# First two u tiles side by side from small loads, spreading products inside later tiles, second B table loaded early

## The chip, the cores and the metric

The kernel runs on one core of a Trainium2 chip. The metric is the time of one execution on the device in microseconds (us), as the median of several runs. The engines are TensorE (PE, with its weight loads PEld), VectorE (DVE), ScalarE (ACT), GpSimd (POOL) and SyncE (SP), which only issues transfers. A profile is one profiled execution; its times count from the start of its span.

## The reference

A decoder block in float32 on 528 tokens (16 meta tokens and 512 of the sequence) of width 1024:

```
xn = rmsnorm(h);  proj = xn @ w_in          # q, k, v, r, a_low, u, z_gla, z_ssm
o  = gla_chunked(q, k, v, log_sigmoid(a_low @ w_gate_up + b_gate) / 16)
y_gla = (rmsnorm(o) * silu(r)) @ w_o_gla
y_s = s5_ssm(u, ...)                         # 64 groups of 16 channels, 64 complex states each
y_ssm = GLU of gelu(y_s) @ w_glu + b_glu
h = h + rmsnorm((sigmoid(z_gla) * y_gla + sigmoid(z_ssm) * y_ssm) @ w_out)
h = h + rmsnorm(square(relu(rmsnorm(h) @ w_ff1)) @ w_ff2)
```

In `s5_ssm` the input matrix of each group is `Bbar = f * B` with complex f and B: `bb_re = fr * br - fi * bi`, `bb_im = fr * bi + fi * br`.

## The kernel before, in words

Every large product is made three times over. A float32 operand is split into a high half (`split_hi`, a ScalarE copy to the reduced type) and a low half (VectorE, operand minus high half), and `mm3` adds hi*hi, hi*lo and lo*hi in PSUM. A weight tile is 1024 x 128: eight k of 128 rows. `raw_w` loads it (tag `wraw`, three buffers, 512 KB) on SyncE's queue, `split_w` makes `whi` and `wlo` (three buffers each). Tokens come in two halves, 0 to 255 and 256 to 527 (`HALVES`), so a tile of one half is 24 matmuls of 256 or 272 columns.

In the first stage VectorE and ScalarE instructions are held in the program's order (`InOrder`), as are PE's (`pinned`); outside of it a scheduler orders the instructions of each engine by its own model of times, and may put later work ahead. `tc.issue_after(ins)` puts what is traced in its block behind `ins` on the same engine.

**Start (lines 452 to 660).** `u` is the first projection wanted. Its first five tiles of 128 columns are computed before the row norms are known: from x times the norm's gain (`rh`, `rl`, made by `taken_raw(k, q)` for one k and one half), and each result is multiplied by the row scale when it is taken from PSUM (`u_took`). The transposed tokens `x_cols0` come in four loads of two k each and the first weight tile in two of four k each, in turn on SyncE's queue; the second weight tile follows whole, then the second half of the tokens, a table for the S5 parameters, the third weight tile, and the token rows (three buffers `xt`). `busy` issues products of a constant tile so that PE has work until then. For each pair of k: two `taken_raw`, then `split_part` of the first weights; after these the first tile's 24 matmuls, then the second weight tile is split, then its 24 matmuls, then both tiles for the second half of the tokens.

`squared(i)` makes the sum of squares of token tile i on ScalarE, in place, and so frees a row buffer in the end; `rooted` makes the reciprocal roots (ScalarE's Sqrt and five small VectorE operations); `spread(q)` is a short PE product that spreads the row scales of half q over all partitions; `rows_of(q)` copies them from PSUM. Then `scaled`, `high` and `low` make the normalized x in halves (`xh`, `xl`), which everything later reads. `spread(0)` stands ahead of the third u tile, `spread(1)` ahead of the fourth. `work(us)` takes small VectorE operations for the S5 parameters from the list `jobs` until their estimated costs are used up.

**Early tiles (lines 663 to 895).** Ten calls of `early_slot(before, after)` follow, numbered 0 to 9 here; call n makes the matmuls of dense tile n (three u tiles, then seven gates of 24 matmuls of 512 columns). Between the high and the low half of the weights for tile n + 2 it does `before` of the jobs, and after the low half `after` of them. The jobs are here the powers of lambda, `b_bar`, the sums of the decay logarithms and so on. Seven of the calls stand in the block whose pools `qc` and `q5` close at lines 894 and 895, three behind it (lines 1251 to 1253).

**Second B table (lines 1242 to 1249).** `BA` holds the first B table, loaded early. Behind the seventh call the pool `b5` of the S5 blocks is open; the loads of the first block's `B` and `lam` are issued on GpSimd, and `other`, the second B table (`b_cols[1]`, 512 KB), is loaded on SyncE's queue into the buffer with the tag M3, which the blocks use later. Three jobs make `BA = BA * fr + other * fi`; four more make the first block's tables M2 and M1 (`tables`), of which M1 reads `B` and `lam`. Then the eight S5 blocks run beside the four heads; block 0 needs BA in `kernels`, its `E` (filled by `turns`, L1106) and `U` (eight loads, L1110) and M1 in `scan`.

Of the kernel before, what the change touches and what calls it, by code (L numbers as in the profile page):

```python
# [50 lines left out]
def hybrid_block(ctx: ExitStack, tc: tile.TileContext, io, out: bass.AP):  # L51
# [29 lines left out]
    def mk(pool, shape, dt=F32, tag=None, **kw):  # L81
        count[0] += 1
        name = f"{tag or 'x'}_{count[0]}"
        size = 1
        for n in shape[1:]:
            size *= n
        if pool not in lined or size % LINE == 0:
            return pool.tile(shape, dt, tag=tag or name, name=name, **kw)
        t = pool.tile([shape[0], -(-size // LINE) * LINE], dt, tag=tag or name, name=name, **kw)[:, :size]
        if len(shape) == 2:  # L90
            return t
        dims = " ".join("abcd"[: len(shape) - 1])
        return t.rearrange(f"p ({dims}) -> p {dims}", **dict(zip("abcd", shape[1:])))
# [23 lines left out]
    V.memset(warm, 1.0)  # L117
    S.activation(warm, warm, AF.Sqrt)
    epst = mk(cst, [P, 1], tag="epst")
# [10 lines left out]
    def bank(tag="sm"):  # L130
        return mk(ps_mm if tag == "mm" else ps_sm, [P, 512], tag=tag)
# [327 lines left out]
    rh, rl = (mk(pxt, [P, KT, LINE + SEQ], F32R, tag=t)[:, :, :NT] for t in ("rh", "rl"))  # L459
    raws, xts, loaded = [mk(wp, [P, KT, P], tag="wraw", bufs=3)], {}, None  # L460

    def behind():
        return tc.issue_after(loaded.ins) if loaded else ExitStack()

    for k in range(0, KT, 2):
        with behind():
            loaded = nc.sync.dma_start(xT[:, k : k + 2, :256], io["x_cols0"][:, k : k + 2])  # L467
        if k % 4 == 0:
            with behind():
                loaded = nc.sync.dma_start(raws[0][:, k : k + 4], w_in[k * P : (k + 4) * P, C_U : C_U + P].rearrange("(k p) n -> p k n", p=P))  # L470
    idle = bank()
# [12 lines left out]
    early = []  # L484
    for kind, i in (("u", 1), ("h", 0), ("h", 4), ("a", 0), ("u", 2), ("x", 0), ("x", 1), ("x", 2), ("x", 3), ("x", 4), ("u", 3), ("u", 4), ("w", 0), ("g", 0), ("u", 5), ("c", 0), ("u", 6), ("u", 7)):
        with behind():
# [84 lines left out]

    def raw_product(w, q, ps):
        a, b = HALVES[q]
        feat_tile(w, rh, rl, a, b, ps[:, : b - a])

# [6 lines left out]
    w0, w1 = (tuple(mk(wp, [P, KT, P], F32R, tag=t, bufs=3) for t in ("whi", "wlo")) for _ in range(2))  # L582
    for k in range(0, KT, 2):
        for i in range(2):
            taken_raw(k + i, 0)
        split_part(w0, raws[0], slice(k, k + 2))
    pair = bank("mm")
    raw_product(w0, 0, pair)
    for k in (0, 4):
        split_part(w1, raws[1], slice(k, k + 4))  # L590
    raw_product(w1, 0, pair[:, 256:])
    for k in range(KT):
        taken_raw(k, 1)
    last = {0: bank("mm"), 1: bank("mm")}
    raw_product(w0, 1, last[0])
    raw_product(w1, 1, last[1])
    w2_ = split_w(raws[2])
    squared(0)
    squared(1)
    rooted(slice(0, 2))  # L600
    V.tensor_copy(tri, trif)
    work(1.6)
    squared(2)
    ps = spread(0)
    rows_of(0, ps)
    pair2 = bank("mm")
    raw_product(w2_, 0, pair2)
    for i in range(2):
        u_took(pair[:, 256 * i : 256 * i + 256], uts[i], 0, True)
    squared(3)  # L610
    squared(4)
    scaled(0, range(0, 4))
    rooted(slice(2, TT + 1))
    w3 = split_w(raws[3])
    scaled(0, range(4, 8))
    high(0, range(0, 4))
    last[2] = bank("mm")
    raw_product(w2_, 1, last[2])
    ps = spread(1)
    low(0, (0, 2))  # L620
    raw_product(w3, 0, pair2[:, 256:])
    w4_hi = split_w_hi(raws[4])
    high(0, range(4, 8))
    rows_of(1, ps)
    w4 = w4_hi, split_w_lo(raws[4], w4_hi)
# [175 lines left out]
    with tc.issue_after(loaded.ins):  # L801
        nc.sync.dma_start(bn, io["b_rows"])
    nc.gpsimd.dma_start(kpad.rearrange("(t g) h l -> (g h) t l", g=GB)[:, :, :112], zpad)
    bar = mk(q5, [P, T8, 2, N], tag="bar")
    fb = mk(q5, [P, 2, N], tag="fb")
    lam = mk(q5, [P, 2, 9, N], tag="lamp")

    def powers_begun():
# [81 lines left out]
    work(2.4)  # L890
    early_slot(2.5, 2.2)
    early_slot(2.2, 100.0)
    assert not jobs
# [349 lines left out]
    first = blocks[0].tables()  # L1243
    other = mk(b5, [P, GB, P], tag="M3", bufs=1).rearrange("p a b -> p (a b)").rearrange("p (g h) -> p g h", h=HG)
    nc.sync.dma_start(other.rearrange("p g h -> p (g h)"), io["b_cols"][1])
    fr, fi = (prm[:, i, :].unsqueeze(2).to_broadcast([P, GRP, HG]) for i in range(2))
    jobs.append((1.2, lambda: V.tensor_mul(BA, BA, fr)))
    jobs.append((1.2, lambda: V.tensor_mul(other, other, fi)))
    jobs.append((1.2, lambda: V.tensor_add(BA, BA, other)))
    jobs.extend((c, lambda: next(first, None)) for c in (2.6, 1.4, 1.2, 2.6))  # L1250
    early_slot(2.2, 2.2)
    early_slot(2.2, 2.2)
# [422 lines left out]
```

## Time and profile before

| | us |
|---|---|
| median of 3 runs | 880.61 (880.41 to 881.18) |
| the profiled execution | 881.0 |
| its span | 879.3 |
| PE busy | 864.8 |
| VectorE busy | 653.0 |
| ScalarE busy | 442.7 |

A row of the timeline is: start, duration, engine, line, operation, output<-inputs, sizes, how many were merged, and in brackets the idle time of the engine before it and what ended it. SPq, ACTq, DVEq and POOLq are the queues in which an engine issues transfers or waits. Most instructions of the first stage have line 79 or 61, those of the helpers that record them, so they are told apart by the names of their tiles: `rh`, `rl` are x times the gain in halves, `whi`, `wlo` the weights in halves, `xrs` the row scales, `M` stands for M1, M2 and M3 (and for `other`, which lies in M3's buffer), `BA` is the B table. A row of the windows has the busy time of each engine in a stretch, the clock that PE was granted as a share of full speed, the busy share of the transfer engines and GB/s.

### The profile page before, as it was taken

The page shows a single profiled execution, that of the slowest core. Times are in us where ns is not written, and L with a number is a line of the kernel's source. Part 1 is how long each engine was busy: PE and PEld are TensorE (multiplying, and loading weights), DVE is VectorE, ACT ScalarE, POOL GpSimd, SP SyncE. Part 2 cuts the span into 40 slices and gives each one's busy share as a digit, 9 for nine tenths or more (in the row PEclk, how much of TensorE's full clock was granted, in tenths as well). Part 3 has the DMA queues.
Part 4 walks back from the last instruction along what each step waited for, and adds up shares of the span by engine and source line. Part 5 has one row for each costly group of instructions (what it writes and reads, how often), then busy time and mean ns, then how long its engine had stood idle before and what let it go on. Part 6 is the DMA issues. An engine that isn't in the chain of part 4 may idle for free.

```text
span 879.3 us, 13267 instructions
## 1 busy us (share of the span) xinstructions
PE 864.8 (98%) x4824; PEld 739.0 (84%) x4824; DVE 653.0 (74%) x1180; ACT 442.7 (50%) x749; POOL 121.8 (14%) x214
## 2 busy tenths in 40 slices
PE   8999899999999999999999999999999999999996
PEld 7998798999988888888888888988888888888885
DVE  6999789969695789956445765576666677688886
ACT  7677356767564545435333544333222236665763
POOL 1123120121213221342000001021112100000001
PEclk9999899999999999999999999999999999999998
DMA  8866785654555766758545761598999967856564
GB/s 289 262 198 190 219 191 135 165 141 133 143 133 149 221 170 190 197 159 278 178 143 169 216 191 52 182 319 291 336 302 305 319 238 223 279 194 195 172 206 144
DMA packets 166841, 180.57 MB, mean 205 GB/s; under 512 B 17992, under 2 KB 126696, under 8 KB 166776
## 3 DMA queue, kind: packets, MB, share of 16 engines
q1 hardware_dynamic: 147720, 117.26, 45.8%
q0 software_dynamic: 17744, 58.52, 19.9%
q10 hardware_dynamic: 1312, 3.94, 1.4%
q8 instruction: 38, 0.62, 0.3%
q14 instruction: 27, 0.22, 0.1%
HBM read 143.74 MB, written 35.95 MB: 204 GB/s over the span
## 4 chain that ended last, share of the span: by engine, by line
PE 92%; DMA 3%; DVE 2%; ACT 2%; SPq 1%; issue 1%; DVEq 0%; POOL 0%
PE mm L61 68%; PE sm L61 23%; PE sm L66 2%; DMA B<-bard 1%; DMA U<-ud 1%; DMA wraw<-in_w_in_dram 1%; ACT ga L79 0%; SPq L1110 0%; DVE b L79 0%; ACT whi L79 0%; ACT L79 0%; DVE c L1596 0%; SPq L467 0%; DVE wlo L79 0%; ACT prm L79 0%
## 5 line engine op out<-in xcount | busy, mean ns | idle before, releaser
L161 ACT ACTIVATE whi<-wraw 128x1024 fp32r<-128x1024 f32 x87 | 92.2, 1059 | 217.0 <-PE mm L61 191.8
L176 DVE TENSOR_TENSOR wlo<-wraw,whi 128x1024 fp32r<-128x1024 f32 x87 | 106.3, 1222 | 103.5 <-ACT whi L161 103.2
L61 PE MATMUL mm<-xh,wlo 128*128 128x512 f32 (+2 forms) x464 | 157.2, 339 | 3.2 <-DVE wlo L79 3.2
L61 PE MATMUL mm<-xh,whi 128*128 128x512 f32 (+2 forms) x464 | 159.9, 345 | 0.0
L61 PE MATMUL mm<-xl,whi 128*128 128x512 f32 (+2 forms) x464 | 156.6, 337 | 0.0
L61 PE MATMUL mm<-hh,whi 128*128 128x512 f32 (+1 forms) x280 | 104.0, 371 | 0.0
L61 PE MATMUL mm<-hl,whi 128*128 128x512 f32 (+1 forms) x280 | 103.8, 371 | 0.0
L61 PE MATMUL mm<-hh,wlo 128*128 128x512 f32 (+1 forms) x280 | 103.8, 371 | 0.0
L61 PEld LDWEIGHTS mm<-xh,wlo 128*128 128x128 f32 x464 | 88.2, 190 | 13.0 <-DVE wlo L79 3.7
L61 PEld LDWEIGHTS mm<-xh,whi 128*128 128x128 f32 x464 | 88.3, 190 | 9.7 <-issue 1.2
L61 PEld LDWEIGHTS mm<-xl,whi 128*128 128x128 f32 x464 | 88.2, 190 | 8.7
L1533 DVE TENSOR_TENSOR wlo<-wraw,whi 128x1024 fp32r<-128x1024 f32 x56 | 68.4, 1222 | 22.4 <-ACT whi L1529 22.1
L61 PE MATMUL sm<-whi,fl 128*128 128x512 f32 x192 | 74.8, 390 | 0.0
L61 PE MATMUL sm<-wlo,fh 128*128 128x512 f32 x192 | 74.8, 390 | 0.0
L61 PE MATMUL sm<-whi,fh 128*128 128x512 f32 x192 | 74.7, 389 | 0.0
L1529 ACT ACTIVATE whi<-wraw 128x1024 fp32r<-128x1024 f32 x56 | 58.7, 1049 | 19.2 <-PE mm L61 11.7
L61 PEld LDWEIGHTS mm<-hh,whi 128*128 128x128 f32 x280 | 52.7, 188 | 9.1
L61 PEld LDWEIGHTS mm<-hh,wlo 128*128 128x128 f32 x280 | 52.7, 188 | 9.0
L61 PEld LDWEIGHTS mm<-hl,whi 128*128 128x128 f32 x280 | 52.7, 188 | 9.0
L161 ACT ACTIVATE fh<-f 128x512 fp32r<-128x512 f32 x48 | 30.3, 631 | 43.4 <-PE sm L61 28.1
L61 PE MATMUL mm<-gh,whi 128*128 128x512 f32 x128 | 49.8, 389 | 0.0
L61 PE MATMUL mm<-gl,whi 128*128 128x512 f32 x128 | 49.8, 389 | 0.0
(408 smaller groups left out, 1773.1 us busy)
## 6 DMA issues: line engine op xcount, KB each, us to landing
wraw<-in_w_ff_dram SPq DMA_DIRECT2D x56, 512.0 KB, 5.7
wraw<-in_w_in_dram SPq DMA_DIRECT2D x47, 512.0 KB, 4.0
w2raw<-in_w_ff_dram POOLq DMA_DIRECT2D x16, 1024.0 KB, 8.9
t2d<-w2t POOLq DMA_DIRECT2D x16, 1024.0 KB, 5.9
wraw<-t2d SPq DMA_DIRECT2D x32, 512.0 KB, 3.7
wraw<-in_w_glu_dram SPq DMA_DIRECT2D x16, 512.0 KB, 4.2
M<-kpad POOLq DMA_DIRECT2D x64, 64.0 KB, 2.7
wraw<-in_w_o_gla_dram SPq DMA_DIRECT2D x8, 512.0 KB, 6.2
```

Source lines behind the costliest of these rows:

```text
L61: ins = nc.tensor.matmul(*args, **kw)
L66: ins = nc.tensor.transpose(*args, **kw)
L161: S.activation(dst, src, AF.Copy, scale=scale)
L176: V.tensor_sub(lo, raw, f32(hi))
L1529: halved = S.activation(bh, raw, AF.Copy)
L1533: V.tensor_sub(bl, raw, f32(bh))
```

## The change

Four things change.

- The first two u tiles are computed side by side: for each k the three matmuls of the first and the three of the second, into two PSUM banks (`side_by_side`), in both halves of the tokens. The first two k of both weight tiles are loaded on ScalarE's queue, the rest on SyncE's between the tokens; the first two k of the tokens come one by one. The weights are split in parts 0 to 1, 2 to 3 and 4 to 7, each after one `taken_raw`. The warming Sqrt of ScalarE, which loads its table, goes behind its two loads.
- `spread(0)` and `spread(1)` go into the third and fourth u tiles, ahead of their k = 3. `rooted` for the later tokens goes behind the fourth weight tile's split and two more scalings. Two results go to the other PSUM tag.
- `other` gets a place of its own in the pool `q5` and is loaded behind `bn` ahead of the early tiles. The three jobs go ahead of what was the seventh call of `early_slot`.
- One call of `early_slot` more stands ahead of the closing of the pools, and one fewer behind it.

```diff
--- before.py
+++ after.py
@@ -115,7 +115,6 @@
 
     warm = mk(cst, [P, 1], tag="warm")
     V.memset(warm, 1.0)
-    S.activation(warm, warm, AF.Sqrt)
     epst = mk(cst, [P, 1], tag="epst")
     V.memset(epst, EPS)
     ident = mk(cst, [P, P], tag="ident")
@@ -457,17 +456,24 @@
     nc.scalar.dma_start(g8, io["g_cols"])
     xT = mk(pxt, [P, KT, NT], tag="xT")
     rh, rl = (mk(pxt, [P, KT, LINE + SEQ], F32R, tag=t)[:, :, :NT] for t in ("rh", "rl"))
-    raws, xts, loaded = [mk(wp, [P, KT, P], tag="wraw", bufs=3)], {}, None
+    raws, xts, loaded = [mk(wp, [P, KT, P], tag="wraw", bufs=3) for _ in range(2)], {}, None
 
     def behind():
         return tc.issue_after(loaded.ins) if loaded else ExitStack()
 
-    for k in range(0, KT, 2):
+    def first_w(queue, i, k, n):
+        return queue.dma_start(raws[i][:, k : k + n], w_in[k * P : (k + n) * P, C_U + i * P : C_U + (i + 1) * P].rearrange("(k p) n -> p k n", p=P))
+
+    first_w(nc.scalar, 0, 0, 2)
+    held = first_w(nc.scalar, 1, 0, 2)
+    with tc.issue_after(held.ins):
+        S.activation(warm, warm, AF.Sqrt)
+    for i, k, n in (("x", 0, 1), ("x", 1, 1), (0, 2, 2), ("x", 2, 2), (1, 2, 2), ("x", 4, 2), (0, 4, 4), (1, 4, 4), ("x", 6, 2)):
         with behind():
-            loaded = nc.sync.dma_start(xT[:, k : k + 2, :256], io["x_cols0"][:, k : k + 2])
-        if k % 4 == 0:
-            with behind():
-                loaded = nc.sync.dma_start(raws[0][:, k : k + 4], w_in[k * P : (k + 4) * P, C_U : C_U + P].rearrange("(k p) n -> p k n", p=P))
+            if i == "x":
+                loaded = nc.sync.dma_start(xT[:, k : k + n, :256], io["x_cols0"][:, k : k + n])
+            else:
+                loaded = first_w(nc.sync, i, k, n)
     idle = bank()
 
     def busy(n, cols=256):
@@ -482,7 +488,7 @@
         return nc.sync.dma_start(xt[:n], io["meta_tokens"] if t == TT else io["x"][0, t * P : (t + 1) * P, :])
 
     early = []
-    for kind, i in (("u", 1), ("h", 0), ("h", 4), ("a", 0), ("u", 2), ("x", 0), ("x", 1), ("x", 2), ("x", 3), ("x", 4), ("u", 3), ("u", 4), ("w", 0), ("g", 0), ("u", 5), ("c", 0), ("u", 6), ("u", 7)):
+    for kind, i in (("h", 0), ("h", 4), ("a", 0), ("u", 2), ("x", 0), ("x", 1), ("x", 2), ("x", 3), ("x", 4), ("u", 3), ("u", 4), ("w", 0), ("g", 0), ("u", 5), ("c", 0), ("u", 6), ("u", 7)):
         with behind():
             if kind == "x":
                 loaded = x_load(i)
@@ -569,9 +575,16 @@
             kk = slice(k, k + 2)
             V.tensor_sub(xl[:, kk, cols], xT[:, kk, cols], f32(xh)[:, kk, cols])
 
-    def raw_product(w, q, ps):
+    def raw_product(w, q, ps, within=None):
         a, b = HALVES[q]
-        feat_tile(w, rh, rl, a, b, ps[:, : b - a])
+        feat_tile(w, rh, rl, a, b, ps[:, : b - a], within=within)
+
+    def side_by_side(ws, q, pss):
+        a, b = HALVES[q]
+        for k in range(KT):
+            for (hi, lo), ps in zip(ws, pss):
+                for i, (w, t) in enumerate(((hi, rh), (hi, rl), (lo, rh))):
+                    PE.matmul(ps[:, : b - a], w[:, k], t[:, k, a:b], start=(k == 0 and i == 0), stop=(k == KT - 1 and i == 2))
 
     def split_part(w, raw, kk):
         split_hi(w[0][:, kk], raw[:, kk])
@@ -580,48 +593,47 @@
     uts = [u_tile() for _ in range(3)] + [mk(qc, [P, T8, NCK], tag=f"ut{i}") for i in (3, 4)]
     busy(5)
     w0, w1 = (tuple(mk(wp, [P, KT, P], F32R, tag=t, bufs=3) for t in ("whi", "wlo")) for _ in range(2))
-    for k in range(0, KT, 2):
-        for i in range(2):
-            taken_raw(k + i, 0)
-        split_part(w0, raws[0], slice(k, k + 2))
-    pair = bank("mm")
-    raw_product(w0, 0, pair)
-    for k in (0, 4):
-        split_part(w1, raws[1], slice(k, k + 4))
-    raw_product(w1, 0, pair[:, 256:])
+    for k in range(KT):
+        taken_raw(k, 0)
+        for w, raw in zip((w0, w1), raws):
+            if k in (0, 2):
+                split_part(w, raw, slice(k, k + 2))
+            elif k == 4:
+                split_part(w, raw, slice(k, KT))
+    firsts = bank("mm"), bank()
+    side_by_side((w0, w1), 0, firsts)
     for k in range(KT):
         taken_raw(k, 1)
     last = {0: bank("mm"), 1: bank("mm")}
-    raw_product(w0, 1, last[0])
-    raw_product(w1, 1, last[1])
+    side_by_side((w0, w1), 1, (last[0], last[1]))
     w2_ = split_w(raws[2])
     squared(0)
     squared(1)
+    V.tensor_copy(tri, trif)
+    work(0.5)
     rooted(slice(0, 2))
-    V.tensor_copy(tri, trif)
-    work(1.6)
+    work(1.3)
     squared(2)
-    ps = spread(0)
-    rows_of(0, ps)
-    pair2 = bank("mm")
-    raw_product(w2_, 0, pair2)
+    pair2, spreads = bank("mm"), []
+    raw_product(w2_, 0, pair2, (3, lambda: spreads.append(spread(0))))
+    rows_of(0, spreads[0])
     for i in range(2):
-        u_took(pair[:, 256 * i : 256 * i + 256], uts[i], 0, True)
+        u_took(firsts[i][:, :256], uts[i], 0, True)
     squared(3)
+    scaled(0, range(0, 4))
+    w3 = split_w(raws[3])
     squared(4)
-    scaled(0, range(0, 4))
+    scaled(0, range(4, 6))
     rooted(slice(2, TT + 1))
-    w3 = split_w(raws[3])
-    scaled(0, range(4, 8))
+    scaled(0, range(6, 8))
     high(0, range(0, 4))
-    last[2] = bank("mm")
+    last[2] = bank()
     raw_product(w2_, 1, last[2])
-    ps = spread(1)
     low(0, (0, 2))
-    raw_product(w3, 0, pair2[:, 256:])
+    raw_product(w3, 0, pair2[:, 256:], (3, lambda: spreads.append(spread(1))))
     w4_hi = split_w_hi(raws[4])
     high(0, range(4, 8))
-    rows_of(1, ps)
+    rows_of(1, spreads[1])
     w4 = w4_hi, split_w_lo(raws[4], w4_hi)
     low(0, (4, 6))
     last[3] = bank()
@@ -799,11 +811,14 @@
     zpad = mk(q5, [P, 8, 112], tag="zpad")
     G.memset(zpad, 0.0)
     with tc.issue_after(loaded.ins):
-        nc.sync.dma_start(bn, io["b_rows"])
+        loaded = nc.sync.dma_start(bn, io["b_rows"])
     nc.gpsimd.dma_start(kpad.rearrange("(t g) h l -> (g h) t l", g=GB)[:, :, :112], zpad)
     bar = mk(q5, [P, T8, 2, N], tag="bar")
     fb = mk(q5, [P, 2, N], tag="fb")
     lam = mk(q5, [P, 2, 9, N], tag="lamp")
+    other = mk(q5, [P, GRP, HG], tag="other")
+    with tc.issue_after(loaded.ins):
+        nc.sync.dma_start(other.rearrange("p g h -> p (g h)"), io["b_cols"][1])
 
     def powers_begun():
         lr, li = lam[:, 0], lam[:, 1]
@@ -889,6 +904,11 @@
     early_slot(2.2, c_rows)
     work(2.4)
     early_slot(2.5, 2.2)
+    fr, fi = (prm[:, i, :].unsqueeze(2).to_broadcast([P, GRP, HG]) for i in range(2))
+    jobs.append((1.2, lambda: V.tensor_mul(BA, BA, fr)))
+    jobs.append((1.2, lambda: V.tensor_mul(other, other, fi)))
+    jobs.append((1.2, lambda: V.tensor_add(BA, BA, other)))
+    early_slot(2.2, 2.2)
     early_slot(2.2, 100.0)
     assert not jobs
     sga.close()
@@ -1241,14 +1261,7 @@
             (r_slot if kind[0] == "r" else o_slot)(m)
     blocks[0].loads(nc.gpsimd)
     first = blocks[0].tables()
-    other = mk(b5, [P, GB, P], tag="M3", bufs=1).rearrange("p a b -> p (a b)").rearrange("p (g h) -> p g h", h=HG)
-    nc.sync.dma_start(other.rearrange("p g h -> p (g h)"), io["b_cols"][1])
-    fr, fi = (prm[:, i, :].unsqueeze(2).to_broadcast([P, GRP, HG]) for i in range(2))
-    jobs.append((1.2, lambda: V.tensor_mul(BA, BA, fr)))
-    jobs.append((1.2, lambda: V.tensor_mul(other, other, fi)))
-    jobs.append((1.2, lambda: V.tensor_add(BA, BA, other)))
     jobs.extend((c, lambda: next(first, None)) for c in (2.6, 1.4, 1.2, 2.6))
-    early_slot(2.2, 2.2)
     early_slot(2.2, 2.2)
     early_slot(2.2, 100.0)
     assert not jobs and next(first, None) is None
```

## The prediction

> **What bounds the kernel now.** I read the page, then the waits of TensorE, then the timeline and the windows around each wait. The page first:
>
> ```profile
> span 879.3 us, 13267 instructions
> PE 864.8 (98%) x4824; PEld 739.0 (84%) x4824; DVE 653.0 (74%) x1180; ACT 442.7 (50%) x749; POOL 121.8 (14%) x214
> PE 92%; DMA 3%; DVE 2%; ACT 2%; SPq 1%; issue 1%; DVEq 0%; POOL 0%
> ```
>
> TensorE (PE) is busy 98% of the span and carries 92% of the chain that ended last. The change keeps its matmuls: it can only take away the few places where PE waits or runs at a lower clock. The longest of its waits (total, times, longest):
>
> ```profile
> PE mm L61 <- DVE wlo L79: 3.2, 1, 3.2
> ```
>
> The others are of 1.3 us and less. This one lies late in the early tiles. PE's timeline, then windows (PE, PEld, DVE, ACT, POOL busy, granted clock, DMA share, GB/s):
>
> ```profile
> 88.22 0.39 PE L61 MATMUL mm<-xh,whi 128*128 128x512 f32 x1
> ...
> 93.66 0.39 PE L61 MATMUL mm<-xh,whi 128*128 128x512 f32 x1
> 93.88 0.39 PE L61 MATMUL mm<-xl,whi 128*128 128x512 f32 x1
> 97.52 0.80 PE L61 MATMUL mm<-xh,wlo 128*128 128x512 f32 x1 [3.25 <-DVE wlo L79]
> ```
>
> ```profile
> 5.75:14.03 8.28, 7.63 (x48) 6.17 (x49) 7.25 (x18) 7.19 (x18) 0.00 (x0) 1.00 1.11 364
> 20.00:22.70 2.70, 2.70 (x26) 2.70 (x26) 2.67 (x13) 2.10 (x5) 0.00 (x0) 1.00 0.81 223
> 97.52:103.20 5.68, 5.68 (x13) 4.46 (x14) 5.58 (x7) 1.06 (x1) 0.00 (x0) 0.50 0.67 199
> ```
>
> Tile 8 starts at 88.22 and tile 9 at 93.66: 24 matmuls in 5.44, 0.227 us each. Tile 9's third matmul, due at 94.11, starts at 97.52: **3.41 us lost**. The third row then shows PE at a granted clock of 0.50. The chain gives what that costs:
>
> ```profile
> 97.52 13.80 PE mm L61 x70
> ```
>
> Those 70 are 22 of 512 columns, 24 of 256 and 24 of 272. At the full clock (0.227 above; 0.113 and 0.1235 from the rows of the start, below) they take 4.99 + 2.72 + 2.96 = 10.68 us: **3.12 us lost**, together 6.5 us. Why VectorE was late:
>
> ```profile
> 84.80 1.45 DVE L79 TENSOR_TENSOR_SCAN b<-mn,ga 128x128 f32<-128x128 f32 x5
> 86.16 1.20 DVE L79 TENSOR_TENSOR wlo<-wraw,whi 128x1024 fp32r<-128x1024 f32 x1
> 87.28 1.21 DVE L79 TENSOR_TENSOR BA<-BA,prm 128x1024 f32<-128x1024 f32 x1
> ...
> 93.97 1.22 DVE L79 TENSOR_TENSOR M<-M,prm 128x1024 f32<-128x1024 f32 x1 [5.27 <-DMA B<-bard]
> 95.11 1.22 DVE L1088 TENSOR_TENSOR M<-CA,Lr 128x1024 f32<-128x1024 f32 x1
> 96.25 1.22 DVE L79 TENSOR_TENSOR wlo<-wraw,whi 128x1024 fp32r<-128x1024 f32 x1
> ```
>
> ```profile
> 83.47 0.54 SPq L1245 DMA_DIRECT2D M<-in_b_cols_dram  x1
> ```
>
> M<-M,prm is `other * fi`. It doesn't read B, so the name of the releaser is only the transfer that ended last nearby; what it reads is `other`, issued at 83.47 and there 10.5 us later. Behind it, in order, stands the low half for tile 9.
>
> As for the clock: PE idled 3.41 us and then had half speed. The Trainium skill, "TensorE: Matmul & The Clock Gate", Part 1, has a window of about 3.4 us without work dropping the clock to 4/8 and as long a busy one giving it back; the trace agrees (0.50 until about 103.2). By that rule no shorter gap of the changed kernel costs clock.
>
> **Part 1, two u tiles side by side.** The rows of the start:
>
> ```profile
> 4.43 0.91 ACT L79 ACTIVATE rh<-xT,g 128x256 fp32r<-128x256 f32 x2 [1.64 <-DMA xT<-in_x_cols_dram]
> 5.28 0.42 ACT L79 ACTIVATE whi<-wraw 128x256 fp32r<-128x256 f32 x1
> 9.06 0.89 DVE L79 SCALAR_TENSOR_TENSOR rl<-xT,g,rh 128x256 fp32r<-128x256 f32 x2 [0.16 <-ACT rh L79]
> 10.01 1.15 ACT L79 ACTIVATE whi<-wraw 128x512 fp32r<-128x512 f32 x2 [0.27 <-DMA wraw<-in_w_in_dram]
> 13.24 0.28 PE L61 MATMUL mm<-rh,wlo 128*128 128x256 f32 x1
> ...
> 13.92 0.28 PE L61 MATMUL mm<-rh,wlo 128*128 128x256 f32 x1
> 14.03 0.28 PE L61 MATMUL mm<-rh,whi 128*128 128x272 f32 x1
> ...
> 19.96 0.60 PE L61 MATMUL sm<-ident,xrs 128*128 128x128 f32 x4
> ```
>
> A 256-column matmul takes (13.92 - 13.24)/6 = 0.113 us, a 272-column one (19.96 - 14.03)/48 = 0.1235. The 48 products of the first half take 5.75 to 14.03 = 8.28 us where 48 x 0.113 = 5.4 would do: 2.8 us are there to gain. Now ScalarE sets the pace: 8 x 0.45 of `rh`, 4 x 0.42 and 2 x 0.58 of weights = 6.4 us, and from 4.4 that is 10.8 without a wait. The same 2 MB come in; w1, then their last part, was used at 10.01; now the last x pair is their end: two `rh` (0.9) to 10.9, the last `rl` to 11.4, and PE, with six matmuls of 0.113 for each of the last k, near 12.6. So PE stands at the second half about **1.4 us earlier** (0.5 to 2.0 by how the small loads land). The two issues moved to ScalarE, about 0.5 each by SyncE's (0.54 above), push its table load back by 1 us; it was idle for 1.64 before its first x at 4.43, so they cost nothing (0.5 if they ran past it). SyncE has nine issues ahead of the next x half instead of seven, 1 us more; the transfers, not the issues, set the pace there.
>
> The Trainium skill, "DMA: Bandwidth & Descriptors", Issuing engines are not separate DMA queues, says that a second issuing queue saves only issue time since the same 16 engines move the bytes. The first row of windows agrees, with a DMA share of 1.11 already from one queue.
>
> **Part 2, spreading inside later tiles.** What the 1.4 us run into:
>
> ```profile
> 18.97 0.39 SPq L167 DMA_DIRECT2D wraw<-in_w_in_dram  x1
> 23.55 1.05 ACT L79 ACTIVATE whi<-wraw 128x1024 fp32r<-128x1024 f32 x1
> 23.61 0.16 DVE L79 TENSOR_SCALAR xrh<-xss 128x3 f32<-128x3 f32 x1
> 24.63 1.22 DVE L79 TENSOR_TENSOR wlo<-wraw,whi 128x1024 fp32r<-128x1024 f32 x1 [0.18 <-ACT whi L79]
> 25.77 1.66 DVE L79 SCALAR_TENSOR_TENSOR xT<-xT,g,xrows 128x256 f32<-128x256 f32 x4
> 26.10 0.93 PE L61 MATMUL sm<-ident,xrs 128*128 128x128 f32 x6
> 26.95 0.39 PE L61 MATMUL mm<-rh,whi 128*128 128x256 f32 x1
> 29.79 0.28 PE L61 MATMUL sm<-rh,whi 128*128 128x272 f32 x1
> ```
>
> The fourth u tile's weights are issued at 18.97, behind the x rows, whose buffers ScalarE frees; nothing in the change brings that forward. From 20.0 to 22.7 the window above moves 223 x 2.7 = 0.60 MB, which is what is left of the meta rows (64 KB) and these 512 KB. So they cannot be used much before 23.2; I take 23.4, against 23.55. High half to 24.45, low half 24.5 to 25.65. PE, 1.4 earlier, is at that tile at 24.75 (before: 26.95 less 1.4 and less the 0.85 of spreading that now comes later) and waits for its low half until 25.7. Three k later, at 26.5, comes spread(1). Its root is moved behind the low half and two scalings (2 x 0.41): 25.65 + 0.8 + 0.9 of root (23.61 to about 24.5) = 27.3. PE waits another 0.8, spreads 0.85, has 15 matmuls of 0.113 left, and starts the next half at 27.3 + 0.85 + 1.7 = 29.85: before 29.79. **The 1.4 us are given back: +0.1 net** (-0.6 if the weights land by 22.8; +0.6 if the root is late). This holds wherever between 12.6 and 14 the second half starts. The waits are of 1 us; those of the start (8.28 less 7.63 in the first window) left the clock at 1.00. VectorE is full there (2.67 of 2.70), so nothing later hides a gain.
>
> **Part 3, the second B table.** The load of `other` goes behind `bn`, before the first early tile: 512 KB, at the 223 to 364 GB/s of the windows 1.4 to 2.4 us of traffic. The weights behind it are split two tiles ahead of their use (11 us), and PE has no wait for them in that stretch: nothing; without that cover, up to 2.4. Its three products (1.14 each) now stand in the slot before: BA*fr ahead of the low half for tile 8, the others ahead of that for tile 9. By the rows: 86.16 + 1.14 + 1.2 = 88.5 for tile 8, which needs it at 88.22 + 0.45 = 88.67: 0 to 0.3, taken as 0.1. For tile 9: 88.4 + 3 x 1.14 = 91.9, needed at 94.11: 2 us to spare. **So 3.41 + 3.12 = 6.5 us go.** What is late next is the first block of the S5 stage:
>
> ```profile
> 97.40:119.50 22.10, 21.98 (x150) 20.03 (x151) 21.86 (x37) 9.28 (x16) 1.08 (x2) 0.87 0.65 179
> ```
>
> ```profile
> 119.75 0.43 DVE L1147 TENSOR_TENSOR v<-sm,E 128x260 f32<-128x260 f32 x1 [0.25 <-PE sm L61]
> ```
>
> VectorE is full from 97.4 to 119.5 (21.86 of 22.1 us), up to the scan's v; BA+ (1.14) leaves this stretch, but the next block's M2 product (L1088, 1.14), which had filled the idle time, comes into it. So v comes near 91.9 + 22.1 = 114.0 where PE, 6.5 earlier, is through at 113.2: **0.8 us given back** (0 if the scheduler puts filler behind v; 1.5 if the block's tables wait for lambda).
>
> **Sum**, against the profiled execution (881.0, span 879.3): start -1.4, given back +1.5, wait at tile 9 -3.4, its clock -3.1, tile 8 +0.1, first block +0.8 = -5.5, so 875.5. That execution was 0.4 above the median of 880.61: **875.1 us**, its own range 873.6 to 876.6.
>
> **Rivals.**
> - *The start keeps its gain and nothing is given back*: -1.4 - 6.5 = **872.7**. For it: the waits of part 2 hang on a landing that I set by a window. Against: 0.60 MB in that window leaves no room.
> - *The wait moves on.* VectorE meets B and lambda instead, in M1, two products further on. B counts as the releaser at 93.97; M1 comes near 97 (91.9, the low half for tile 10 and the first three products). If lambda lands at 101 or later, M1, three operations more and the low half behind them (5 x 1.14) pass what tile 11 needs (93.66 + 5.44 + 5.7 = 104.8), and the scan goes back by 2 to 4 us: **878**. Against it: 512 KB fewer are on the way then.
> - *Slower: the first block's tiles land on `other`.* With its own place in the pool that closes before the first block, 4 KB per partition, `other` lies by the tile sizes where that block's E and U then go; so SyncE's U loads wait for BA+ (90.7). SyncE issues in order:
>
> ```profile
> 87.39 0.38 SPq L167 DMA_DIRECT2D wraw<-in_w_in_dram  x1
> 99.34 1.06 ACT L79 ACTIVATE whi<-wraw 128x1024 fp32r<-128x1024 f32 x1 [4.89 <-DMA wraw<-in_w_in_dram]
> ```
>
> If a U load gets ahead of the weights for tile 10 (which went out ahead of L1245), these leave at 91 and, with the 12 us that the weights above took (87.39 to 99.34), land at 103; split (1.06 + 1.2) they are there at 105.4, and tile 10 wants them at 99.3: 6.1 us of wait and 3.1 of clock take all back and 3 more: 880.6 - 5.5 + 9.2 = **884.3**. It decides from a landing near 100 on. Against it: weights come earlier in program order than U, and their usual landing was 4.0 us:
>
> ```profile
> wraw<-in_w_in_dram SPq DMA_DIRECT2D x47, 512.0 KB, 4.0
> ```
>
> - *It does nothing*: only if `other` still arrived late; it is issued eight tiles ahead, so I leave 2% for that and for cancelling.
>
> **How the numbers follow.** Forecast 0.55, full gain 0.15, wait moved on 0.16, slower 0.12, no change 0.02. The first three are faster: 0.86. 0.2% (1.8 us) is about what a measurement of this kernel can tell from no change. The range goes from the full gain (872.4) to above the moved wait (879.2): 0.86 less some of the tails.
>
> **What would show it.** Right: no wait of PE above 1.5 us after the start, clock 1.00 from 90 to 110; the first 272-column matmul near 12.6; two waits of 0.5 to 1 us between 24 and 28; the half after spread(1) still near 29.8; the three BA products between 86 and 91 and no idle VectorE there. Wrong: the half after spread(1) well before 29 (the full gain), VectorE idle before M1 (moved on), SyncE waiting between 83 and 91 with weights behind it (slower), or a clock below 1.00 at 25 to 30 from the two waits.

## The result and the profile after

| | before | after |
|---|---|---|
| median of 20 runs each, us | 880.03 (879.00 to 881.28) | 879.34 (877.96 to 886.63) |
| the profiled execution, us | 881.0 | 879.83 |

The ratio of after to before is 1.0002, with a 95% interval from 0.9989 to 1.0014: no difference that can be measured, where 875.1 was predicted. It goes by the means (880.29 and 880.15), the table has the medians: the runs of after spread more widely than those of before, with five of the twenty above 881.9.

The page of the kernel after, and the waits of PE (what waited, for what: total, times, longest):

```profile
span 878.0 us, 13276 instructions
PE 863.7 (98%) x4824; PEld 738.3 (84%) x4824; DVE 653.3 (74%) x1180; ACT 444.8 (51%) x751; POOL 121.9 (14%) x214
PE 87%; DVE 5%; DMA 4%; issue 1%; ACT 1%; SPq 1%; ACTq 0%; DVEq 0%
```

```profile
PE sm L66 <- DVE e_gk L997: 1.5, 1, 1.5
PE mm L61 <- DVE wlo L79: 1.5, 2, 0.8
...
PE mm L61 <- ACT whi L79: 1.1, 1, 1.1
PE sm L61 <- DVE xrs L79: 0.5, 1, 0.5
```

The wait of 3.2 us is gone, but four shorter groups of waits stand in the list (that for `e_gk` was 1.05 before), and PE's share of the chain has gone from 92% to 87%. Where they lie is seen in PE's timeline of after, and, for comparison, in two rows of before that were not shown yet (the start of tile 10, and the first wait of head 0 for its decayed keys `e_gk`):

```profile
13.71 0.29 PE L61 MATMUL mm<-rh,whi 128*128 128x272 f32 x1
27.19 0.39 PE L61 MATMUL mm<-rh,wlo 128*128 128x256 f32 x1 [0.76 <-DVE wlo L79]
28.82 1.00 PE L61 MATMUL sm<-ident,xrs 128*128 128x128 f32 x6 [0.54 <-DVE xrs L79]
31.56 0.28 PE L61 MATMUL sm<-rh,whi 128*128 128x272 f32 x1
100.86 0.28 PE L61 MATMUL mm<-xh,whi 128*128 128x256 f32 x1
108.58 0.39 PE L61 MATMUL mm<-xh,whi 128*128 128x256 f32 x1 [1.09 <-ACT whi L79]
109.84 0.38 PE L61 MATMUL mm<-xh,wlo 128*128 128x256 f32 x1 [0.75 <-DVE wlo L79]
132.01 0.62 PE L66 MATMUL sm<-ident,e_gk 128*16 128x128 f32 x4 [1.52 <-DVE e_gk L997]
```

```profile
105.27 0.28 PE L61 MATMUL mm<-xh,whi 128*128 128x256 f32 x1
133.28 0.40 PE L66 MATMUL sm<-ident,e_gk 128*16 128x128 f32 x2 [1.05 <-DVE e_gk L977]
```

PE's place in after, less that in before, at each mark:

| mark | before | after | difference |
|---|---|---|---|
| second half of the tokens | 14.03 | 13.71 | -0.32 |
| half after spread(1) | 29.79 | 31.56 | +1.77 |
| tile 10 | 105.27 | 100.86 | -4.41 |
| wait for `e_gk` | 133.28 | 132.01 | -1.27 |
| span | 879.3 | 878.0 | -1.3 |

So four things happened: the start won 0.3 instead of 1.4 us; 2.1 us were given back up to spread(1); 6.2 us were won between there and tile 10, as forecast; and 3.1 us of that were lost again between tile 10 and head 0's keys, where 0.8 had been forecast. After 132 nothing changes any more.

Between tile 10 and `e_gk` the timeline of after shows a new stall. VectorE first, then ScalarE, then SyncE's queue:

```profile
103.42 0.69 DVE L974 TENSOR_TENSOR d<-b 128x512 f32<-128x512 f32 x1 [5.37 <-DMA b<-bd]
...
104.63 1.22 DVE L79 TENSOR_TENSOR M<-B,lam 128x1024 f32<-128x1024 f32 x1
```

```profile
103.46 1.28 ACT L970 ACT_TABLE_LOAD   x1 [10.16 <-DMA b<-bd]
104.87 0.62 ACT L970 ACTIVATE e_gq<-b 128x512 f32<-128x512 f32 x1
105.69 1.28 ACT L79 ACT_TABLE_LOAD   x1
107.48 1.05 ACT L79 ACTIVATE whi<-wraw 128x1024 fp32r<-128x1024 f32 x1
```

```profile
90.73 0.53 SPq L964 DMA_DIRECT2D b<-bd  x1
91.31 12.40 SPq L1130 DMA_DIRECT2D U<-ud  x8
103.81 1.02 SPq L166 DMA_DIRECT2D wraw<-in_w_in_dram  x2
```

`d<-b` and `e_gq<-b` are head 0's decay work (`decays`, `query_decay`). It isn't held in the program's order, and in after the scheduler has put it ahead of work that is: VectorE stands 5.4 us before a subtraction that needs `b`, with M1 behind it, and ScalarE 10.2 us before the table load of an exponential, with a second table load and tile 11's high half behind that. `b` was issued at 90.73 and is there at 103.4, 12.7 us later. In before the same subtraction stood behind all of the early work, at 110.98.

### The profile page after: what moved, and what is told of

It reads as the page before. It is cut to its first block, busy times and chain, and to the rows that moved or that the text cites. A ratio compares the mean times of both kernels' runs of the same rounds, so it can differ in the third digit from the quotient of the medians.

```text
span 878.0 us, 13276 instructions
## 1 busy us (share of the span) xinstructions
PE 863.7 (98%) x4824; PEld 738.3 (84%) x4824; DVE 653.3 (74%) x1180; ACT 444.8 (51%) x751; POOL 121.9 (14%) x214
## 4 chain that ended last, share of the span: by engine, by line
PE 87%; DVE 5%; DMA 4%; issue 1%; ACT 1%; SPq 1%; ACTq 0%; DVEq 0%
PE mm L61 63%; PE sm L61 22%; DMA wraw<-in_w_in_dram 2%; PE sm L66 2%; DMA b<-bd 1%; DVE wlo L79 1%; DMA xt<-in_x_dram 1%; DVE b L79 1%; DVE c L1609 0%; SPq L488 0%; ACT whi L79 0%; DVE M L79 0%; DVE E L79 0%; DVE t L79 0%; ACT mn L79 0%
```

## The experiments

A ratio is to the kernel before on the same chip, with its 95% interval.

| run | what it is | median, us | before, us | ratio |
|---|---|---|---|---|
| table_only | part 3 alone | 878.23 | 880.00 | 0.9979 (0.9968 to 0.9990) |
| start_only | parts 1 and 2 | 881.46 | 880.00 | 1.0024 (1.0014 to 1.0034) |
| side_only | part 1 alone | 880.24 | 880.00 | 1.0004 (0.9995 to 1.0013) |
| spread_only | part 2 alone | 880.63 | 880.00 | 1.0008 (0.9999 to 1.0017) |
| table_held | part 3, decays held back | 876.37 | 880.22 | 0.9956 (0.9943 to 0.9969) |
| table_place | part 3, table elsewhere | 874.17 | 880.22 | 0.9929 (0.9918 to 0.9941) |
| side_first | part 1, spread(0) inside | 880.32 | 880.22 | 1.0003 (0.9994 to 1.0011) |
| combo | side_first and table_place | 874.07 | 880.22 | 0.9931 (0.9919 to 0.9943) |
| after_place | the whole change, table elsewhere | 875.54 | 880.64 | 0.9941 (0.9929 to 0.9954) |
| after_u3 | the same, fourth weights earlier | 874.55 | 880.64 | 0.9932 (0.9919 to 0.9946) |

### The parts by themselves

Part 3 alone is the diff from the load of `bn` on, made in the kernel before; parts 1 and 2 are what stands ahead of it in the diff.

> The kernel before with part 3 alone (second B table in its own place, its three products one slot earlier). Theory 'two separate losses' (the start costs 1.8 us in its own right, the wait at tile 9 really goes, and the first S5 block gives about 3 us of it back): tile 10 starts some 6 us earlier than before, 2 to 3 us are lost at tile 11 and in the first block, and 877 us against 880 is left (-3, ratio 0.9965). Rival 'a later bound takes everything' (VectorE or the heads' chain ends at the same time whatever PE does before): within 0.8 us of the kernel before.

> The kernel before with parts 1 and 2 (side by side, spreading inside later tiles), the second B table as before. Theory 'two separate losses': the half after spread(1) starts near 31.5 instead of 29.8, the wait at tile 9 stands as before, the end is 1 to 1.8 us later (881.3 to 882). Rival 'hidden': the wait at tile 9 hangs on a transfer that is issued at the same time, so it shrinks by what PE comes later, and the time is that of before (within 0.5 us).

Part 3 alone wins 1.8 us, where 3 were expected, and the start alone costs 1.5 us; together they cancel, which is the result above. "Two separate losses" holds (though the half after spread(1) came at 30.45 with the start alone, not at 31.5), "a later bound takes everything" and "hidden" fall. Part 3 alone has the stall of VectorE (5.1 us ahead of `d<-b`, at 101.15) and the waits at tile 11 (0.79 and 0.76) as after has. It also shows where the rest goes. Its wait for `e_gk`, and the windows from there in the kernel with part 3 alone (2.02 us of wait), then in after (1.52 us):

```profile
130.23 0.64 PE L66 MATMUL sm<-ident,e_gk 128*16 128x128 f32 x3 [2.02 <-DVE e_gk L985]
...
126.00:140.00 14.00, 11.98 (x68) 9.47 (x67) 13.84 (x30) 7.96 (x14) 0.00 (x0) 0.88 0.68 191
```

```profile
126.00:140.00 14.00, 12.48 (x78) 9.98 (x77) 13.84 (x28) 7.81 (x14) 0.62 (x2) 1.00 0.71 183
```

A mean clock of 0.88 over 14 us is 14 x 0.12 x 2 = 3.4 us at half speed, which costs 1.7 us on top of the wait; after a wait of 1.52 us the clock stayed at 1.00. Not every execution of part 3 alone need have this: the profiled one took 879.31 us, 1.1 above the median.

### The start

Part 1 alone keeps before's order behind the two tiles; part 2 alone keeps before's loads and first two tiles:

```diff
-    ps = spread(0)
-    rows_of(0, ps)
-    pair2 = bank("mm")
-    raw_product(w2_, 0, pair2)
+    pair2, spreads = bank("mm"), []
+    raw_product(w2_, 0, pair2, (3, lambda: spreads.append(spread(0))))
+    rows_of(0, spreads[0])
...
+    scaled(0, range(0, 4))
+    w3 = split_w(raws[3])
     squared(4)
-    scaled(0, range(0, 4))
+    scaled(0, range(4, 6))
     rooted(slice(2, TT + 1))
-    w3 = split_w(raws[3])
-    scaled(0, range(4, 8))
+    scaled(0, range(6, 8))
...
```

> The kernel before with part 1 alone: the two tiles side by side from the small loads, all spreading and roots where they were. Theory 'the loads' (the start's loads come in later, so the row buffers come free later and the fourth u tile's weights land near 24.8 instead of 23.5): the fourth tile's weights are again used near 24.8 and the half after spread(1) starts 1 to 1.8 us later than before. Rival 'the root' (the loss comes from the root and the spreading moved behind the fourth tile's split): weights used by 24.0, the half after spread(1) within 0.4 us of before.

> The kernel before with part 2 alone: loads and first two tiles as before, spreading inside the third and fourth u tile and the roots later. Theory 'the loads': weights of the fourth tile used at 23.5 as before and the half after spread(1) within 0.4 us of before (29.4 to 30.2). Rival 'the root': the half after spread(1) 0.8 to 1.8 us later than before, with a wait for the row scales of 0.5 us or more ahead of spread(1).

With part 1 alone the second half started at 12.90, 1.1 earlier than before; PE then waited 0.80 for the row scales of spread(0), and the half after spread(1) came at 29.93 (+0.14). The time is before's. With part 2 alone that half came at 30.38 (+0.59). ScalarE's rows show why, first of part 2 alone, then of before:

```profile
23.69 1.06 ACT L79 ACTIVATE whi<-wraw 128x1024 fp32r<-128x1024 f32 x1 [0.58 <-DVE xT L79]
24.66 1.04 ACT L79 ACTIVATE xt<-xt 16x1024 f32<-16x1024 f32 x1
...
25.82 0.30 ACT L79 ACTIVATE xra<-xss,epst 128x3 f32<-128x3 f32 x1
```

```profile
22.18 1.04 ACT L79 ACTIVATE xt<-xt 16x1024 f32<-16x1024 f32 x1
...
23.35 0.30 ACT L79 ACTIVATE xra<-xss,epst 128x3 f32<-128x3 f32 x1
23.55 1.05 ACT L79 ACTIVATE whi<-wraw 128x1024 fp32r<-128x1024 f32 x1
```

In before the meta rows' squares and the root stand ahead of the fourth weights and use the time until they land; in the change they stand behind them, so the root is taken 2.5 us later. (The first row names VectorE's `xT` as what ended the wait; the split reads only `wraw`, whose landing is the likelier end.) Both expectations come out half: each part costs a little, by "the root" with before's loads, by "the loads" where the weights land later too (used at 24.21 with part 1 alone). Apart, the two are within what can be told from no change; together they cost 1.5 us.

Next, part 1 with only spread(0) moved into its tile and the root where it was:

> Part 1 alone with spread(0) inside the third tile (ahead of its k = 3) and everything else in the order of before: root and spread(1) stand ahead of the fourth tile. Theory 'row scales' (part 1 alone started the second half 1.1 us earlier and lost it in a wait of 0.8 us for spread(0)'s row scales; the moved root and spread(1) cost 0.6 by themselves): the half after spread(1) starts near 29.0 and the time is 0.8 below before, 879.2. Rival 'the weights' (the fourth tile's weights cap the start whatever is ahead): a wait of PE of 0.5 us or more for the fourth tile's low half, the half after spread(1) at 29.8 or later, 880 or more.

PE had no wait over 0.1 us from 7 to 35 us, and the half after spread(1) came at 29.07, as "row scales" says (29.0). The time didn't follow: 880.32. But the profiled execution was the fastest of the twelve (878.96 to 883.16), so its start need not be that of the others. Whether an earlier start is lost later or wasn't there in most runs stays open.

### What stalls VectorE before M1

One run holds head 0's decay work behind the ordered instructions; another moves the second B table out of `q5` into the gates' pool `pga`, away from the space that the first block takes over:

```diff
+    still = mk(cst, [P, 1], tag="still")
+    marks = V.memset(warm, 1.0), S.copy(still, epst)
     V, S = nc.vector, nc.scalar
...
-            this.decays()
+            with tc.issue_after(marks[0].ins), tc.issue_after(marks[1].ins):
+                this.decays()
```

```diff
-    other = mk(q5, [P, GRP, HG], tag="other")
+    other = mk(pga, [P, GRP, HG], tag="other")
```

> Part 3 alone, with the first head's decay work (subtraction of b, its exponentials) held behind the last of VectorE's and ScalarE's ordered instructions of the early tiles. Theory 'decays ahead' (what stalled VectorE for 5 us before M1 and put two table loads ahead of tile 11's high half was only that unordered work, waiting for its own load): VectorE goes on with M1 when lambda is there (near 99 instead of 101.8), no wait at tile 11 (1.55 us before), the scan and the wait for e_gk come 2 us earlier; 875.5 to 877 us. Rival 'the transfers' (B and lambda land as late themselves): VectorE idles before M1 until 101, the wait at tile 11 stays, and the time is that of part 3 alone, 878.2 +- 0.8.

> Part 3 alone, but the second B table lies in the pool of the gates on the other side, so that the first block's E and U no longer land on it. Theory 'place' (E and U on the table's place kept the eight U loads back, b's load went ahead of them, and with it the decays went ahead of M1): U loads start near 84, ahead of tile 11's weights, b's load behind tile 12's; VectorE has no decay work before M1, no wait at tile 11; 875.5 to 877 us. Rival 'place is nothing': the same stall of VectorE before M1 and 878.2 +- 0.8.

Rows of the kernel with the decays held (VectorE, then ScalarE):

```profile
98.75 1.23 DVE L79 TENSOR_TENSOR M<-B,lam 128x1024 f32<-128x1024 f32 x1 [0.96 <-DMA lam<-lamd]
...
106.34 1.22 DVE L79 TENSOR_TENSOR wlo<-wraw,whi 128x1024 fp32r<-128x1024 f32 x1 [3.56 <-ACT whi L79]
```

```profile
101.34 1.28 ACT L958 ACT_TABLE_LOAD   x1 [10.03 <-DMA b<-bd]
102.64 0.63 ACT L958 ACTIVATE e_gq<-b 128x512 f32<-128x512 f32 x1
...
105.27 1.05 ACT L79 ACTIVATE whi<-wraw 128x1024 fp32r<-128x1024 f32 x1
```

M1 starts 3.6 us earlier than with part 3 alone (102.36), as soon as lambda is there: lambda and B were not late, the subtraction ahead of M1 was. The wait at tile 11 is still there, though (0.84 and 0.76), against the expectation: `query_decay` is traced apart from `decays` and wasn't held, so ScalarE still stood before `e_gq` with tile 11's high half behind it. The 1.9 us that this run wins over part 3 alone come later: its wait for `e_gk` is 1.11 instead of 2.02 and costs no clock. No run holds `query_decay` back as well.

With the table elsewhere both are gone (SyncE's queue, VectorE, ScalarE):

```profile
84.69 0.82 SPq L1118 DMA_DIRECT2D U<-ud  x2
...
97.64 0.34 SPq L952 DMA_DIRECT2D b<-bd  x1
```

```profile
97.74 1.22 DVE L79 TENSOR_TENSOR M<-B,lam 128x1024 f32<-128x1024 f32 x1
...
101.56 1.22 DVE L79 TENSOR_TENSOR wlo<-wraw,whi 128x1024 fp32r<-128x1024 f32 x1
```

```profile
97.66 1.06 ACT L79 ACTIVATE whi<-wraw 128x1024 fp32r<-128x1024 f32 x1 [3.39 <-DMA wraw<-in_w_in_dram]
```

U's loads start at 84.7 as in before, `b` is issued 9 us later than with part 3 alone, the decays stand behind tile 11's split, and PE has no wait over 0.1 us between 20 and 126 us. The only edit is the place: 878.23 becomes 874.17, 0.7% below before and better than expected (875.5 to 877). The signs of theory "place" are all there, but the reason that it gives, E and U on the table's place, is not. Rows of part 3 alone (ScalarE, SyncE's queue, VectorE):

```profile
84.64 0.32 ACT L1114 COPY E<-E 128x144 f32<-128x144 f32 x1 [0.35 <-DVE E L79]
```

```profile
89.30 12.15 SPq L1118 DMA_DIRECT2D U<-ud  x8
```

```profile
89.39 1.23 DVE L79 TENSOR_TENSOR BA<-BA,other 128x1024 f32<-128x1024 f32 x1
```

E is first written (from the table E8) 4.7 us before BA+ reads `other` for the last time, and as early as with the table elsewhere (84.69). The first U load leaves before BA+ begins. So neither waits for the table's buffer; in the built program that buffer shares its bytes with the second buffer of M2, and not with E or U. What the place did change is the order: on SyncE's queue U's loads stand behind `b`, and on GpSimd's the first load of B leaves at 87.80 instead of 82.83. In the built programs the block's first work stands right behind the last instruction that uses the pool `q5`: that is BA+ with the table in it, and the last product of E8 without. That the scheduler goes by the pool, not by the bytes, is the likely reason; it is argued, and no run shows it.

### Putting it together

> side_first and table_place together. If both theories hold and the gains add: 0.8 + 3 to 4.5 us below before, 874.7 to 876.2. Rival 'a later bound' (the first head's keys, e_gk, come at the same time whatever stands before): no faster than table_place alone (within 0.5 us), with the wait for e_gk longer by what the start gained.

> The whole change, with the second B table in the gates' pool as in the part-3 run that had it there (874.2 us). Theory 'the start costs' (parts 1 and 2 together come 1 to 1.5 us late and nothing later hides it): 875.2 to 875.9, the half after spread(1) at 30.4 to 31.6. Rival 'hidden' (a later wait of PE swallows what the start loses): within 0.5 us of 874.2.

> The kernel of after_place with the fourth u tile's weights requested ahead of the last token rows and the meta rows instead of behind them. Theory 'the weights cap' (the fourth tile waits for its low half, which waits for weights that stand behind rows whose buffers come free late): its high half by 22.5 instead of 24 to 24.8, no wait of PE for that low half, the half after spread(1) 0.5 to 1.2 us earlier than in after_place, and the time as much lower. Rival 'the root caps' (spread(1) waits for the later tokens' row scales, whose rows now land no earlier): a wait of 1 us or more ahead of spread(1), the half after it at most 0.3 us earlier.

combo is as fast as table_place (874.07), which is the time of "a later bound". The other sign of that rival is missing: its wait for `e_gk` is 0.37 us, not longer than table_place's 0.76. As its start came out no earlier in its profile (29.66, table_place 29.61), the run doesn't decide between the two. The whole change with the table elsewhere takes 875.54: 5.1 us below before, and 1.1 (by the ratios) to 1.4 us above table_place, which is again the cost of the start; the two intervals overlap, so this figure is a weak one. The order of two loads in after_u3,

```diff
-    for kind, i in (... ("x", 2), ("x", 3), ("x", 4), ("u", 3), ("u", 4), ...):
+    for kind, i in (... ("x", 2), ("u", 3), ("x", 3), ("x", 4), ("u", 4), ...):
```

brings 1.0 us (its five runs lie between 874.09 and 874.88, four of after_place's five between 875.52 and 875.72; the intervals of the ratios overlap). ScalarE's row of after_u3, then of after_place, and from the start of after_place a wait of PE and a window (columns as in the prediction):

```profile
23.40 1.04 ACT L79 ACTIVATE whi<-wraw 128x1024 fp32r<-128x1024 f32 x1
```

```profile
24.42 1.06 ACT L79 ACTIVATE whi<-wraw 128x1024 fp32r<-128x1024 f32 x1 [0.38 <-DMA wraw<-in_w_in_dram]
```

```profile
7.34 0.39 PE L61 MATMUL sm<-rh,whi 128*128 128x256 f32 x1 [1.30 <-ACT whi L79]
```

```profile
9.00:11.00 2.00, 2.00 (x12) 2.00 (x11) 2.00 (x5) 2.00 (x6) 0.00 (x0) 0.50 1.08 386
```

In after_u3 the fourth weights are no longer waited for (their high half comes at 23.40, where 22.5 was expected), and the half after spread(1) starts at 30.12 instead of 31.18. These two profiles alone don't show that the weights did it. In after_place PE waited 1.30 us at the start and then had half the clock: the mean from 0 to 15 us is 0.89, which is 15 x 0.11 x 2 = 3.3 us at half speed, some 1.6 us lost. So its second half began at 14.71, that of after_u3 at 13.37, and PE waited for the fourth low half in neither. But 30.12 is also earlier than in the four other profiles with this start (30.45 to 31.56). A wait of 0.55 for the row scales is left, the root's. So the weights count and the root comes next; what each costs isn't separated.

Two more profiled executions, of the start alone and of after:

> Parts 1 and 2 alone once more, for a second look at the start. Theory 'landing spread' (the same code comes out 1 us apart from execution to execution by how the small first loads land): the second half of the tokens starts between 12.9 and 13.9 and everything up to the half after spread(1) moves with it. Rival 'fixed': 12.92 and 30.45 again, within 0.15.

> The changed kernel once more, for a second look. Theory 'landing spread': the second half of the tokens starts between 12.9 and 13.9 (13.71 in the first look), the half after spread(1) between 30.4 and 31.6; the stall of VectorE before M1 and the waits at tile 11 are there again. Rival 'fixed': 13.71 and 31.56 within 0.15.

These executions took 881.87 and 880.92 us. The start alone gave 13.50 and 30.90 (12.92 and 30.45 in start_only), after 12.79 and 30.48 (13.71 and 31.56 above): "fixed" falls, though 12.79 is just outside of what "landing spread" expected. In the mean of the five profiles with this start and this order of loads (after_place has 14.71 and 31.18) the second half begins at 13.5, or 13.2 without after_place and its half clock, and the half after spread(1) at 30.9; the four with the old start and the old spreading (before, table_only, table_held, table_place) give 13.9 and 29.6. So the side-by-side start wins 0.4 to 0.6 us, and the way to spread(1) loses it and 1.2 to 1.3 more. In after_look the stall before M1 and the waits at tile 11 were there again, and the wait for `e_gk` was 2.50 us, with 0.88 in the window from 126 to 140.

## Why the prediction was wrong

**The forecast of 875.1 failed by its start and by the first block; the wait at tile 9 was right.** Of the 5.5 us forecast for the profiles 4.2 are missing: 2.3 in the first block, 1.1 at the start, 0.6 on the way to spread(1), 0.2 up to tile 10. By its steps:

- *Wait at tile 9 and its clock, -6.5, with +0.1 at tile 8.* Right in mechanism and size for these two executions: -6.18 between the half after spread(1) and tile 10. The three BA products stand at 87.91, 90.16 and 91.41, the low half for tile 9 at 92.56, PE doesn't wait, and the clock is whole:

```profile
90.00:105.00 15.00, 15.00 (x84) 13.08 (x83) 9.60 (x13) 4.60 (x9) 2.28 (x4) 1.00 0.80 179
```

  The clock's term was read from a costly execution. The same window of before and of part 1 alone:

```profile
90.00:105.00 15.00, 11.75 (x40) 9.15 (x39) 10.93 (x12) 2.37 (x5) 0.56 (x1) 0.77 0.77 227
```

```profile
90.00:105.00 15.00, 11.76 (x45) 9.08 (x44) 10.96 (x12) 3.05 (x7) 0.64 (x2) 0.89 0.78 229
```

  15 x 0.23 x 2 = 6.9 us of half clock in the first, 15 x 0.11 x 2 = 3.3 us in the second, after waits of 3.25 and 3.08 us. Of the six profiles that have this wait two show 0.77 (before, start_look) and four 0.89 (start_only, side_only, spread_only, side_first). So the term is 3.1 us in two of the six and about 1.6 in four. That the size came out here is luck of the profile: with the shorter dip the same change wins 1.5 us less.

- *Start, -1.4.* Only -0.32 (-0.4 in the mean, -0.6 without after_place). The step that failed is "from 4.4 that is 10.8 without a wait": ScalarE waited for parts of the two weight tiles three times, 2.1 us in all, and the last `rh` of the half ended at 11.6 instead of 10.9.

```profile
5.06 0.42 ACT L79 ACTIVATE whi<-wraw 128x256 fp32r<-128x256 f32 x1 [0.91 <-DMA wraw<-in_w_in_dram]
6.11 0.42 ACT L79 ACTIVATE whi<-wraw 128x256 fp32r<-128x256 f32 x1 [0.63 <-DMA wraw<-in_w_in_dram]
...
9.80 0.63 ACT L79 ACTIVATE whi<-wraw 128x512 fp32r<-128x512 f32 x1 [0.54 <-DMA wraw<-in_w_in_dram]
10.34 1.29 ACT L79 ACTIVATE rh<-xT,g 128x256 fp32r<-128x256 f32 x3
```

- *Given back, +1.5, net +0.1.* The mechanism was named (low half first, root next, both after PE), the sizes were not: net +1.77. "I take 23.4" for the fourth weights was the mis-sized term: in after they are used at 24.81, in the other profiles with this order at 23.6 to 24.4, which moves the low half and, behind it, the root. The prediction placed the root on VectorE and didn't see that the change also puts it behind the weights in ScalarE's order: root at 26.94, where before had it at 23.35. (26.95 less 1.4 and 0.85 is 24.70, not 24.75; nothing hangs on that.)

- *First block, +0.8.* This failed most: 3.1 us. The step "v comes near 91.9 + 22.1 = 114.0" took VectorE's order as given, with at most "filler" to move behind v. In after v came at 122.73 (before 119.75): head 0's decays, which stand late in that stretch in before, had moved ahead of M1, with `b` issued ahead of U's loads and 12.7 us on its way. table_place shows it: with the table elsewhere the stall goes and v comes at 117.35.

- *The rivals.* The one with E and U on `other`'s place named the table's place, with a chance of 0.12, but neither the reason (E and U didn't wait for BA+, see the rows of part 3 alone) nor the way: tile 10's weights did leave in time (tile 10 had no wait), tile 12's were the ones behind U (103.81), and the price was paid through the order of the decays. "The wait moves on" named the place (M1, tile 11) and a price near the result (878), for a wrong reason: lambda was there by 98.75 in table_held. "Full gain" didn't come: in after ScalarE waited 1.78 us for the fourth weights.

- *"By that rule no shorter gap of the changed kernel costs clock."* Wrong: waits of 2.02 and 2.50 us for `e_gk` cost 3.4 us of half clock each (0.88 over 14 us), and in after_place one of 1.30 at the start cost about as much, while 1.52 in after cost none. The Trainium skill, "TensorE: Matmul & The Clock Gate", Part 1, asks for a whole idle window of about 3.4 us; gaps of 1.30, 2.02 and 2.50 us here did it already. That it also calls the window free-running would fit the one or two windows of half clock after nearly the same wait; no run here tests it.

The two table loads ahead of tile 11's high half took 1.28 us each (at 103.46 and 105.69 in after), and the instruction behind each began 1.30 after its load began (104.76 and 106.99). The Trainium skill, "ScalarE: Activation LUTs", What ACT_TABLE_LOAD costs, gives the same 1.28 and a drain of 1.38 more for a switch; no drain is seen here.

## What to carry to other kernels

A buffer that is moved into another pool can change the order of work that never touches it: compare the order of the loads and of each engine's work before and after, and not only the tiles on its bytes. One moved tile was worth 4 us here. Where ordered and unordered work share an engine, look for what may be put ahead of the ordered work, and ask when its data really lands. A gain taken from one execution that contains a clock dip should be given with the shorter dip too.

## What was not expected of the hardware

- A short wait can cost the clock, and its length alone doesn't decide: 1.30, 2.02 and 2.50 us did, each time for 3.3 to 3.4 us at half speed, 1.52 us did not. A wait of 3.1 to 3.6 us cost 3.3 us of half clock in four profiles and 6.9 in two.
- The load of `b` took 12.7 us from its issue at 90.73 until it was used at 103.42, with the eight U loads behind it on the same queue.
- The same start code came out between 12.79 and 14.71 at the second half of the tokens, from execution to execution. The waits for the first small loads differ: in after_place ScalarE had one of 1.73 us, PE 1.30 behind it, and the half clock that followed is 1.6 of the 14.71.
- The longest run of after, 886.63 us, had a mean clock of 0.989, the profiled one (879.83 us) 0.997: 0.008 of 878 us is 7.0 us, as much as the 6.8 between them. Where the clock was lost no trace shows, and 883.14 us at 0.996 isn't explained by it.
